# Last 12 of 22 k tiles of the second feed-forward product: seven products of quarters in place of eight

## The chip, the cores and the metric

One core of a Trainium2 chip runs the whole program. The metric is the device time of one execution in microseconds (us); the kernel before takes 709.41 us (median of 3 runs, 708.23 to 709.94). Engines are named as in the profile: PE is the matrix engine (PEld its weight loads), DVE the vector engine, ACT the scalar engine, POOL the GpSimd engine, SP the engine that issues most DMAs.

## The reference

One decoder layer on x of 512 tokens by 1024 channels: two token mixers (a convolution and a forgetting attention) with an output projection, then a feed-forward block. The change touches the last line:

```
x  = x + merged @ w_out                     # mixers
h2 = rmsnorm(x, g_ffn)
gu = h2 @ w_ffn_in                          # 1024 -> 2 x 2816
x  = x + (silu(gu[:, :2816]) * gu[:, 2816:]) @ w_ffn_out     # 2816 -> 1024
```

Everything is float32. A product is made of three passes in the rounded type that PE takes (fp32r): an operand is split in a high part (rounded) and a low part (the rest), and high x high, high x low and low x high are added up in PSUM (`mm3`, `split`).

## The kernel before

Programs for the five engines are written in one order by hand (a manual schedule); each engine takes its instructions in that order and waits on semaphores. Two wrappers, `V` and `T`, stand for DVE and PE, so all their instructions have line L147.

**First feed-forward product.** It is already made in quarters, seven products for eight (Winograd's form), for 11 column groups m of 256 hidden channels in each half. `seq` lists the products (m, p), and for each `one(n)` runs `product` (24 matmuls of 256 columns) and `combine`, which takes results out of PSUM: c11, c12 and c22 hold partial results, and `act` the silu times gate, transposed (128 hidden channels by 512 tokens) for 22 tiles. The last five products are those of m = 10: P6, P5, P7, P3, P4. P7 and P4 add into the same PSUM bank X: after P7 DVE reads X (`c<-acc,c`), and P4 may only then go on adding to it. P4's result is read by `act<-c,acc`.

**Second product** (`for k in range(NF)`). Its 22 k tiles of 128 hidden channels each add to all eight PSUM banks (4 token tiles by 2 halves of the 1024 output columns), 24 matmuls of 512 columns a tile, 528 in all. PSUM has two tags of four banks, `acc` and `mx`, and the banks are taken in the order acc, acc, mx, mx, acc, acc, mx, mx; the sixth is the X of m = 10. For tile k, `down_load` brings 128 rows of w_ffn_out (`wd`, tag raw), `down_split` makes `wdh` (ACT) and `wdl` (DVE), and `act_split` makes `ah` (ACT) and `al` (DVE) of one `act` tile. The weights have three buffers of each tag, so the split for tile k + 2 waits until tile k - 1 is done. The first three loads and splits stand between the last five products of `seq`. In the last tile each finished bank is added to x1 (`x<-x,acc`, `x<-x,mx`) and stored.

**Memory.** `slot` (26 tiles, tag s2) holds mixers' tiles, c22 and act; `f4` (22 tiles of 4 KB a partition) holds operands of the first product and then ah and al, at 2 KB of their 4 KB.

Of the kernel before, what the change touches and what calls it, by code (L numbers as in the profile page):

```python
# [27 lines left out]
NF = DFF // P  # L28
# [7 lines left out]
def hybrid_layer(ctx, tc, x, g_mix, w_in, b_forget, w_dw, b_dw, g_ln, b_ln, w_conv_out,  # L36
# [3 lines left out]
    nc = tc.nc  # L40
    A, G = nc.scalar, nc.gpsimd

    x, out = x[0], out[0]
    w_in, w_conv_out, w_attn_out = w_in[0], w_conv_out[0], w_attn_out[0]
    w_out, w_ffn_in, w_ffn_out = w_out[0], w_ffn_in[0], w_ffn_out[0]

    keep = ctx.enter_context(tc.tile_pool(name="keep", bufs=1))
    wp = ctx.enter_context(tc.tile_pool(name="wp", bufs=2))  # L50
    big = ctx.enter_context(tc.tile_pool(name="big", bufs=1))
    sm = ctx.enter_context(tc.tile_pool(name="sm", bufs=4))
    ps = ctx.enter_context(tc.tile_pool(name="ps", bufs=4, space=bass.MemoryType.PSUM))
    side = tc.alloc_tile_pool(name="side", bufs=1, side="right", reuse_waits="tile")
    ctx.enter_context(tc.manual_schedule())

# [4 lines left out]
        return ps.tile([P, n], F32, tag="mx", name="mx")  # L61

    def slot(dt=F32, name="s2"):
        return big.tile([P, 542], dt, tag="s2", bufs=26, name=name)

    def g8(dt=F32, name="g8"):
        return side.tile([P, 4, 512], dt, tag="g8", bufs=5, name=name)
# [93 lines left out]
    V, T = Clocked(nc.vector, v_adds), Clocked(nc.tensor, t_adds)  # L161
# [450 lines left out]
    for i in range(2):  # L612
        a_ = side.tile([P, NT, 196], F32R, name=f"sq{i}")
# [222 lines left out]
    x1 = []  # L836
# [116 lines left out]
    B11, B21, B22, T1, T2, T3, T4 = range(7)  # L953
# [73 lines left out]
        b_lo(T4, t4)  # L1027
        b_lo(B22, b22)

    act = [None] * NF  # L1030
    X, Y, Z = {}, {}, {}

    def product(m, p):
        hi, lo = ops_.pop((m, p))
        bh, bl = bop[B_OF[p]]
        new = p in (1, 2, 5)
        if p == 1:
            X[m] = acc()
        elif p == 2:
            Z[m] = mx()  # L1040
        elif p == 5:
            Y[m] = mx()
        o = Z[m] if p == 2 else Y[m] if p in (3, 5) else X[m]
        for f in range(2):
            fs = slice(f * P, f * P + P)
            for w in range(3):
                for k in range(KH):

                    first = new and f + w + k == 0
                    T.matmul(o[:, f * 256:f * 256 + 256], (hi, hi, lo)[w][:, k, fs], (bh, bl, bh)[w][:, k, :],  # L1050
                             start=first, stop=w == 2 and k == KH - 1, skip_group_check=not (new and f == 0))

    c11, c12, c22 = {}, {}, {}

    def combine(m, p):
        if p == 1:
            c11[m] = wk(name="c11")
            A.copy(c11[m], X[m])
        elif p == 2:
            V.tensor_tensor(c11[m], Z[m], c11[m], op=ALU.add)  # L1060
            A.activation(c11[m], c11[m], AF.Silu)
        elif p == 5:
            c22[m] = slot(name="c22")[:, :S]
            A.copy(c22[m], Y[m])
        elif p == 6:
            c12[m] = wk(name="c12")
            A.copy(c12[m], X[m])
        elif p == 7:
            V.tensor_tensor(c22[m], X[m], c22[m], op=ALU.add)
        elif p == 4:  # L1070
            for i in range(2):
                if act[2 * m + i] is None:
                    act[2 * m + i] = slot(name="act")[:, :S]
                hs = slice(i * 256, i * 256 + 256)
                V.tensor_tensor(act[2 * m + i][:, :256], c11[m][:, hs], X[m][:, hs], op=ALU.mult)
        elif p == 3:
            V.tensor_tensor(c12[m], Y[m], c12[m], op=ALU.add)
            A.activation(c12[m], c12[m], AF.Silu)
            for i in range(2):
                if act[2 * m + i] is None:  # L1080
                    act[2 * m + i] = slot(name="act")[:, :S]
                hs = slice(i * 256, i * 256 + 256)
                V.tensor_tensor(act[2 * m + i][:, 256:], c12[m][:, hs], c22[m][:, hs], op=ALU.mult)

    def prep_first():

# [15 lines left out]
    def one(n):  # L1102
        product(*seq[n])
        combine(*seq[n])


    down, acts = {}, {}

    def d_rows(k):
        return w_ffn_out[k * P:(k + 1) * P, :]  # L1110

    def down_load(k):
        if k < NF:
            raw = wp.tile([P, D], F32, tag="raw", bufs=3, name="wd")
            nc.sync.dma_start(raw, d_rows(k))
            down[k] = raw

    def down_split(k):
        if k < NF:
            raw = down[k]  # L1120
            hi = wp.tile([P, D], F32R, tag="whi", bufs=3, name="wdh")
            lo = wp.tile([P, D], F32R, tag="wlo", bufs=3, name="wdl")
            split(hi, lo, raw)
            down[k] = hi, lo

    def act_split(k):
        if k < NF:
            hi, lo = f4(F32R, "ah"), f4(F32R, "al")
            hi, lo = (t.rearrange("p k c -> p (k c)")[:, :S] for t in (hi, lo))
            split(hi, lo, act[k])  # L1130
            acts[k] = hi, lo


    for m in range(NP):
# [30 lines left out]
    for n in range(NS):  # L1165
        early = n < 3
        if early:
            for fn, args in todo[n]:
                fn(*args)
        for th in tokens.get(n, ()):  # L1170
            th()
        if not early:
            for fn, args in todo[n]:
                fn(*args)
        for m, key in loads.get(n, ()):
            f_load(m, key)
        one(n)
        if n >= NS - 5:
            i = n - NS + 5
            if i < 3:  # L1180
                down_load(i)
            if 0 < i < 4:
                down_split(i - 1)
            if 1 < i < 4:
                act_split(i - 2)
    banks = [(acc, acc, mx, mx)[i % 4]() for i in range(8)]
    for k in range(NF):
        down_load(k + 3)
        if k > 0:
            down_split(k + 2)  # L1190
        act_split(k + 2)
        hi, lo = down[k]
        for i in range(8):
            t, c = divmod(i, 2)
            ts, cs = slice(t * P, (t + 1) * P), slice(c * 512, (c + 1) * 512)
            mm3(banks[i], acts[k][0][:, ts], acts[k][1][:, ts], hi[:, cs], lo[:, cs], k == 0, k == NF - 1)
            if k == NF - 1:
                V.tensor_tensor(x1[t][:, cs], x1[t][:, cs], banks[i], op=ALU.add)
                nc.sync.dma_start(out[t * P:(t + 1) * P, cs], x1[t][:, cs])
    side.release()  # L1200


# [23 lines left out]
```

## Time and profile before

| | us |
|---|---|
| median of 3 runs | 709.41 |
| the profiled execution, device time | 708.81 |
| its span, first to last instruction | 707.0 |
| PE busy | 694.7 |
| DVE busy | 459.9 |
| ACT busy | 371.6 |
| POOL busy | 123.3 |

The profile follows one execution; times in it are counted from its first instruction. A row of the timeline gives start, duration, engine, line, operation, output and inputs, and in brackets how long the engine had been idle and who ended it. Ends of matmuls are modelled: two matmuls that follow each other overlap in the rows, so their rate is read from their starts. `wd`, `wdh`, `wdl` are a tile of w_ffn_out, its high and its low part; `ah`, `al` those of the activations; `c` any of c11, c12, c22.

### The profile page before, as it was taken

The page shows a single profiled execution, that of the slowest core. Times are in us where ns is not written, and L with a number is a line of the kernel's source. Part 1 is how long each engine was busy: PE and PEld are TensorE (multiplying, and loading weights), DVE is VectorE, ACT ScalarE, POOL GpSimd, SP SyncE. Part 2 cuts the span into 40 slices and gives each one's busy share as a digit, 9 for nine tenths or more (in the row PEclk, how much of TensorE's full clock was granted, in tenths as well). Part 3 has the DMA queues.
Part 4 walks back from the last instruction along what each step waited for, and adds up shares of the span by engine and source line. Part 5 has one row for each costly group of instructions (what it writes and reads, how often), then busy time and mean ns, then how long its engine had stood idle before and what let it go on. Part 6 is the DMA issues. An engine that isn't in the chain of part 4 may idle for free. (4 is left out here: it accounts for less than half of the span.)

```text
span 707.0 us, 10716 instructions
## 1 busy us (share of the span) xinstructions
PE 694.7 (98%) x4264; PEld 614.8 (87%) x4264; DVE 459.9 (65%) x736; ACT 371.6 (53%) x585; POOL 123.3 (17%) x138
## 2 busy tenths in 40 slices
PE   6999999999999999999999999999999999999997
PEld 5988879888888888887889999999999987888886
DVE  5579985988773568497677677667667663333333
ACT  5424546487788677553567465665555552223320
POOL 1302257243333221210001011111110100000000
PEclk9999999999999999999999999999999999999999
DMA  8438999366656611295016568777667463332203
GB/s 257 95 104 172 186 188 184 91 131 125 120 120 122 141 68 60 89 328 177 1 61 131 137 150 179 150 160 162 155 145 158 61 176 93 105 101 90 89 31 119
DMA packets 67124, 92.13 MB, mean 130 GB/s; under 512 B 3281, under 2 KB 46289, under 8 KB 67074
## 3 DMA queue, kind: packets, MB, share of 16 engines
q1 hardware_dynamic: 47810, 65.58, 30.5%
q0 software_dynamic: 18976, 25.35, 22.6%
q8 instruction: 33, 0.54, 0.3%
q10 hardware_dynamic: 288, 0.52, 0.2%
q14 instruction: 17, 0.14, 0.1%
HBM read 89.34 MB, written 2.10 MB: 129 GB/s over the span
## 5 line engine op out<-in xcount | busy, mean ns | idle before, releaser
L212 ACT CAST whi<-wraw 128x1024 fp32r<-128x1024 f32 (+1 forms) x52 | 54.4, 1049 | 54.6 <-PE acc L147 35.4
L147 DVE SCALAR_TENSOR_TENSOR cv<-apad,prm,cv 128x512 f32<-128x512 f32 x120 | 83.1, 764 | 0.0
L147 PE MATMUL acc<-hT_hi,whi 128*128 128x512 f32 (+1 forms) x208 | 75.6, 384 | 0.7 <-ACT hT_hi L77 0.7
L147 DVE TENSOR_TENSOR wdl<-wd,wdh 128x1024 fp32r<-128x1024 f32 x22 | 27.0, 1226 | 74.5 <-ACT wdh L77 74.5
L147 PE MATMUL acc<-hT_hi,wlo 128*128 128x512 f32 (+1 forms) x208 | 73.1, 371 | 0.0
L147 PE MATMUL acc<-hT_lo,whi 128*128 128x512 f32 (+1 forms) x208 | 73.0, 370 | 0.0
L147 DVE TENSOR_TENSOR wl<-wA,wh 128x1024 fp32r<-128x1024 f32 x46 | 56.1, 1222 | 20.0 <-ACT wh L928 19.6
L928 ACT CAST wh<-wA 128x1024 fp32r<-128x1024 f32 x66 | 68.1, 1046 | 1.0 <-DVE wA L147 0.6
L77 ACT CAST wdh<-wd 128x1024 fp32r<-128x1024 f32 x22 | 23.0, 1048 | 79.0 <-PE mx L147 69.3
L924 POOL DMA_DIRECT2D wl<-in_w_ffn_in_dram x20 | 25.7, 1286 | 181.8 <-PE mx L147 105.5
L147 PE MATMUL acc<-bl,wh 128*128 128x256 f32 x352 | 56.3, 282 | 0.0
L147 PE MATMUL acc<-bh,wh 128*128 128x256 f32 x352 | 56.2, 281 | 0.0
L147 PE MATMUL acc<-bh,wl 128*128 128x256 f32 x352 | 56.1, 281 | 0.0
L147 DVE TENSOR_TENSOR wlo<-wraw,whi 128x1024 fp32r<-128x1024 f32 x28 | 34.3, 1223 | 22.1 <-ACT whi L212 21.3
L147 PEld LDWEIGHTS acc<-bl,wh 128*128 128x128 f32 x352 | 48.0, 188 | 0.1
L147 PEld LDWEIGHTS acc<-bh,wh 128*128 128x128 f32 x352 | 47.9, 188 | 0.1
L147 PEld LDWEIGHTS acc<-bh,wl 128*128 128x128 f32 x352 | 47.9, 188 | 0.0
L218 POOL DMA_DIRECT2D wlo<-in_w_in_dram x24 | 29.1, 1213 | 89.1 <-ACT wlo L216 72.0
L147 PEld LDWEIGHTS acc<-hT_hi,wlo 128*128 128x128 f32 x208 | 38.0, 191 | 7.2
L147 PE MATMUL acc<-wlo,hT_hi 128*128 128x512 f32 (+2 forms) x128 | 43.4, 339 | 0.4 <-DMA wlo<-in_w_in_dram 0.4
L147 PEld LDWEIGHTS acc<-hT_hi,whi 128*128 128x128 f32 x208 | 38.1, 193 | 6.5 <-ACT hT_hi L77 1.1
L147 PE MATMUL acc<-whi,hT_lo 128*128 128x512 f32 (+2 forms) x128 | 43.4, 339 | 0.0
(222 smaller groups left out, 1675.1 us busy)
## 6 DMA issues: line engine op xcount, KB each, us to landing
wA<-in_w_ffn_in_dram SPq DMA_DIRECT2D x44, 512.0 KB, 3.8
wraw<-in_w_in_dram SPq DMA_DIRECT2D x26, 512.0 KB, 3.9
wlo<-in_w_in_dram POOLq DMA_DIRECT2D x22, 512.0 KB, 7.9
wd<-in_w_ffn_out_dram SPq DMA_DIRECT2D x22, 512.0 KB, 3.3
wl<-in_w_ffn_in_dram POOLq DMA_DIRECT2D x20, 512.0 KB, 8.4
wraw<-in_w_in_dram SPq DMA_DIRECT2D x16, 256.0 KB, 3.7
wraw<-in_w_out_dram SPq DMA_DIRECT2D x8, 512.0 KB, 6.2
wraw<-in_w_attn_out_dram SPq DMA_DIRECT2D x4, 512.0 KB, 3.4
```

Of the source, the lines that this page charges most:

```text
L77: A.copy(hi, src)
L147: return f(out, *args, **kw)
L212: A.copy(hi, raw)
L218: G.dma_start(lo[:, :, at:at + d["n"]], w_rows(d, c0), accum_op=ALU.add)
L924: G.dma_start(lo, w_quarter(m, *WHERE[SRC[p]]), accum_op=ALU.add)
L928: A.copy(hi, wq[m, SRC[p]])
```

## The change

The 22 k tiles are now 10 plain tiles (KS) and three groups q of four (NQ = 3). In a group the activations (512 tokens by 512 channels) and the weights (512 by 1024) are cut in quarters, and seven products of quarters (P1, P5, P6, P2, P7, P3, P4 for q = 0, 1, 2 each: 21 steps of 12 matmuls of 512 columns) give what eight would. Sums of quarters (S1 to S4 of activations, T1 to T4 of weights) are made by DVE, in place except S1 and T1. Quarters of w_ffn_out are loaded as `dB..` tiles during the plain tiles. Each step's operands are prepared three steps ahead: `dh` and the high part of `da` by ACT, the low part of `da` and `dl` by DVE. For P2 and P3 the low part `dlo` is made five steps ahead by a negated copy (ACT) and a DMA from POOL that adds the quarter again. Results stay in PSUM over steps: X for P1, P6, P7, P4, Y for P5 and P3, Z for P2; after the last group `add_out` adds them to x1.

`act` becomes 11 tiles of two k tiles each, in a new pool on the bytes of the `slot` pool, which is released after product n = 6. So the silu-times-gate product is one instruction of 128x2x256 where there were two of 128x256, and `act_split` works on 128x1024 for two k tiles. For m < 2 c22 is taken from X after P7 instead of from Y after P5.

```diff
-    act = [None] * NF
+    act = [None] * NP
+    def t512(name):
+        return pools["act"].tile([P, 512], F32, tag="t512", bufs=5, name=name)
+    def act_of(m): ...
+            act[m] = pools["act"].tile([P, 2, 512], F32, tag="act", bufs=NP, name="act")
...
-        elif p == 5:
-            c22[m] = slot(name="c22")[:, :S]
+        elif p == 5 and m > 1:
+            c22[m] = t512("c22")
...
         elif p == 7:
-            V.tensor_tensor(c22[m], X[m], c22[m], op=ALU.add)
+            if m < 2:
+                c22[m] = t512("c22")
+                A.copy(c22[m], X[m])
+                V.tensor_tensor(c22[m], Y[m], c22[m], op=ALU.add)
+            else:
+                V.tensor_tensor(c22[m], X[m], c22[m], op=ALU.add)
         elif p == 4:
-            for i in range(2): ...
-                V.tensor_tensor(act[2 * m + i][:, :256], c11[m][:, hs], X[m][:, hs], op=ALU.mult)
+            V.tensor_tensor(act_of(m)[:, :, :256], two(c11[m]), two(X[m]), op=ALU.mult)
...
-    def act_split(k):
-        if k < NF:
-            hi, lo = f4(F32R, "ah"), f4(F32R, "al")
-            split(hi, lo, act[k])
+    NQ = 3
+    KS = NF - 4 * NQ
+    def act_split(m):
+        if 2 * m < KS:
+            acts[m] = f2(F32R, "ah"), f2(F32R, "al")
+            split(*acts[m], act[m])
...
+    Q_SUM = {"T1": ("B12", "B11", "T1"), "T2": ("B22", "T1", "T1"), "T3": ("B22", "B12", "B12"), "T4": ("B21", "T1", "B21"),
+             "S1": ("A21", "A22", "S1"), "S2": ("S1", "A11", "A11"), "S3": ("A11", "A21", "A21"), "S4": ("A12", "A11", "A12")}
...
+    A_SRC = {1: "A11", 2: "A12", 3: "A12", 4: "A22", 5: "S1", 6: "A11", 7: "A21"}
+    B_SRC = {1: "B11", 2: "B21", 3: "B22", 4: "B21", 5: "T1", 6: "T1", 7: "B12"}
+    d_seq = [(p, q) for p in (1, 5, 6, 2, 7, 3, 4) for q in range(NQ)]
+    def wq_slot(dt, name):
+        tag = ("raw", "raw", "whi", "wlo", "raw", "whi", "wlo", "whi", "wlo")[d_n[0] % 9]
...
+    def q_neg(p, q):
+        lo_q[p, q] = f2(F32R, "dlo")
+        A.activation(lo_q[p, q], dq[q, B_SRC[p]], AF.Copy, scale=-1.0)
+        G.dma_start(lo_q[p, q], q_rows(q, B_SRC[p]), accum_op=ALU.add)
+    def q_ops(p, q):
+        w = dq[q, B_SRC[p]]
+        hi = wq_slot(F32R, "dh")
+        lo = lo_q[p, q] if (p, q) in lo_q else wq_slot(F32R, "dl")
+        a_op = f2(F32R, "da")
+        A.copy(hi, w)
+        A.copy(two(a_op[:, 0, :]), quarter(q, A_SRC[p]))
+        V.tensor_tensor(two(a_op[:, 1, :]), quarter(q, A_SRC[p]), two(a_op[:, 0, :].bitcast(F32)), op=ALU.subtract)
+        if (p, q) not in lo_q:
+            V.tensor_tensor(lo, w, hi.bitcast(F32), op=ALU.subtract)
+    def q_step(p, q):
+        bank = {1: "X", 2: "Z", 3: "Y", 4: "X", 5: "Y", 6: "X", 7: "X"}[p]
...
+        for i in range(2):
+            for kk in range(2):
+                for w in range(3):
+                    a_ = a_op[:, w == 2, kk * 256 + i * P:kk * 256 + i * P + P]
+                    T.matmul(dbank[bank][i], a_, (hi, lo, hi)[w][:, kk, :], ...)
+            if q == NQ - 1: ... add_out(t, c, dbank[bank][i], p in (2, 3, 7, 4))
...
-            if 1 < i < 4:
-                act_split(i - 2)
+            if i in (1, 3):
+                act_split(i // 2)
...
+        d_plan(KS - 2 if q < 2 else KS - 1, q_ops, 1, q)
+        d_plan(KS - 1, q_sum, q, "S2")
+        d_plan(KS + q, q_ops, 5, q)
+        d_plan(KS + 1 + q, q_sum, q, "T2")
+        d_plan(KS + d_at[2, q] - 5, q_neg, 2, q)
+        d_plan(KS + d_at[3, q] - 5, q_neg, 3, q)
+        for p in (6, 2, 7, 3, 4):
+            d_plan(KS + d_at[p, q] - 3, q_ops, p, q)
...
-    for k in range(NF): ...
-        act_split(k + 2)
+    for k in range(KS): ...
+        if k % 2 == 0 and k > 0:
+            act_split(k // 2 + 1)
+        for fn, args in d_todo[k]:
+            fn(*args)
...
+    for n, (p, q) in enumerate(d_seq):
+        for fn, args in d_todo[KS + n]:
+            fn(*args)
+        q_step(p, q)
```

The first place is DVE between the last products of the first feed-forward product and the second. Before (`c_6171` is c22 of m = 10, read from X after P7; `c_6138` is c12 after P3; `c_5978` is c11, multiplied with P4's result in `acc`):

```order
L147 TENSOR_TENSOR wdl<-wd,wdh 128x1024
L147 TENSOR_TENSOR c_6171<-acc,c_6171 128x512
L147 TENSOR_TENSOR wdl<-wd,wdh 128x1024
L147 TENSOR_TENSOR al<-act,ah 128x512
L147 TENSOR_TENSOR c_6138<-mx,c_6138 128x512
L147 TENSOR_TENSOR act<-c_6138,c_6171 128x256 x2
L147 TENSOR_TENSOR wdl<-wd,wdh 128x1024
L147 TENSOR_TENSOR al<-act,ah 128x512
L147 TENSOR_TENSOR act<-c_5978,acc 128x256 x2
```

The same place on DVE after the change (`c_6148` is c22, `c_6115` c12, `c_5958` c11):

```order
L149 TENSOR_TENSOR wdl<-wd,wdh 128x1024
L149 TENSOR_TENSOR al<-act,ah 128x1024
L149 TENSOR_TENSOR c_6148<-acc,c_6148 128x512
L149 TENSOR_TENSOR wdl<-wd,wdh 128x1024
L149 TENSOR_TENSOR c_6115<-mx,c_6115 128x512
L149 TENSOR_TENSOR act<-c_6115,c_6148 128x2x256
L149 TENSOR_TENSOR wdl<-wd,wdh 128x1024
L149 TENSOR_TENSOR al<-act,ah 128x1024
L149 TENSOR_TENSOR act<-c_5958,acc 128x2x256
```

The first low part of the activations, now twice as long, has moved up in front of the read of X for c22; the second one, also twice as long, stands as before in front of the read of P4's result.

The second place is DVE where the plain tiles end and the steps begin, after the change; before, the eight `x` rows were the kernel's last (`x_0` to `x_3` are x1's token tiles, `da`, `dl` operands of P1 and P5, `dT` sums of weights):

```order
L149 TENSOR_TENSOR da_6592<-act_6051,da_6592 128x512
L149 TENSOR_TENSOR dl_6591<-dB11_6337,dh_6590 128x1024
L149 TENSOR_TENSOR act_6051<-dS1_6412,act_6051 128x2x256
L149 TENSOR_TENSOR x1_0_3298<-x1_0_3298,acc_6254 128x512
L149 TENSOR_TENSOR x1_0_3298<-x1_0_3298,acc_6255 128x512
L149 TENSOR_TENSOR x1_1_3300<-x1_1_3300,mx_6256 128x512
L149 TENSOR_TENSOR x1_1_3300<-x1_1_3300,mx_6257 128x512
L149 TENSOR_TENSOR x1_2_3302<-x1_2_3302,acc_6258 128x512
L149 TENSOR_TENSOR x1_2_3302<-x1_2_3302,acc_6259 128x512
L149 TENSOR_TENSOR x1_3_3304<-x1_3_3304,mx_6260 128x512
L149 TENSOR_TENSOR x1_3_3304<-x1_3_3304,mx_6261 128x512
L149 TENSOR_TENSOR da_6632<-dS1_6334,da_6632 128x512
```

The first two adds set free the two banks that P1 writes, and operands of P1 and a sum stand in front of them; all eight stand in front of the operands of P5.

## Rows read from the trace of the kernel before

**Rows 1.** The page: busy time of engines, and the chain that ended last

```profile
PE 694.7 (98%) x4264; PEld 614.8 (87%) x4264; DVE 459.9 (65%) x736; ACT 371.6 (53%) x585; POOL 123.3 (17%) x138
...
PE 16%; DVE 1%; issue 0%
```

**Rows 2.** Busy us (and instructions) by stretch: PE, PEld, DVE, ACT, POOL, then clock, DMA

```profile
300.00:320.00 20.00, 20.00 (x89) 16.21 (x88) 17.99 (x22) 11.97 (x15) 3.07 (x5) 1.00 0.94 322
380.00:400.00 20.00, 20.00 (x171) 20.00 (x170) 12.44 (x16) 11.47 (x14) 2.57 (x2) 1.00 0.79 179
450.00:500.00 50.00, 50.00 (x424) 50.00 (x423) 35.87 (x40) 27.68 (x34) 5.13 (x4) 1.00 0.75 164
584.00:704.00 120.00, 119.28 (x513) 96.20 (x513) 40.72 (x47) 29.83 (x38) 0.00 (x0) 1.00 0.26 87
```

**Rows 3.** Timeline, second product's beginning and end (start us, us, engine, line, operation)

```profile
578.92 0.39 PE L147 MATMUL acc<-wdh,ah 128*128 128x512 f32 x1
...
582.15 0.40 PE L147 MATMUL acc<-wdh,al 128*128 128x512 f32 x1
...
583.95 0.51 PE L147 MATMUL acc<-wdh,ah 128*128 128x512 f32 x1 [1.40 <-DVE act L147]
...
702.62 1.38 DVE L147 TENSOR_TENSOR x<-x,mx 128x512 f32<-128x512 f32 x2
...
702.88 0.40 PE L147 MATMUL mx<-wdh,al 128*128 128x512 f32 x1
```

**Rows 4.** Timeline, last products of the first feed-forward product, DVE, ACT and PEld

```profile
573.89 1.04 ACT L928 CAST wh<-wA 128x1024 fp32r<-128x1024 f32 x1
574.02 1.23 DVE L147 TENSOR_TENSOR wdl<-wd,wdh 128x1024 fp32r<-128x1024 f32 x1 [2.50 <-ACT wdh L77]
...
575.16 0.68 DVE L147 TENSOR_TENSOR c<-acc,c 128x512 f32<-128x512 f32 x1
...
575.96 0.54 PEld L147 LDWEIGHTS acc<-bh,wh 128*128 128x128 f32 x4
...
576.26 1.05 ACT L77 CAST wdh<-wd 128x1024 fp32r<-128x1024 f32 x1 [1.32 <-PE mx L147]
...
577.34 1.22 DVE L147 TENSOR_TENSOR wdl<-wd,wdh 128x1024 fp32r<-128x1024 f32 x1 [1.49 <-ACT wdh L77]
...
580.34 1.03 ACT L77 CAST wdh<-wd 128x1024 fp32r<-128x1024 f32 x1
...
581.40 1.23 DVE L147 TENSOR_TENSOR wdl<-wd,wdh 128x1024 fp32r<-128x1024 f32 x1 [0.18 <-ACT wdh L77]
...
582.55 0.68 DVE L147 TENSOR_TENSOR al<-act,ah 128x512 fp32r<-128x512 f32 x1
...
583.15 0.75 DVE L147 TENSOR_TENSOR act<-c,acc 128x256 f32<-128x256 f32 x2
```

**Rows 5.** Groups of instructions from 584 us on: count, busy us, mean ns, idle before

```profile
L147 DVE TENSOR_TENSOR wdl<-wd,wdh 128x1024 fp32r<-128x1024 f32 x19 | 23.3, 1226 | 70.3 <-ACT wdh L77 70.3
L77 ACT CAST wdh<-wd 128x1024 fp32r<-128x1024 f32 x19 | 19.9, 1048 | 75.9 <-PE mx L147 68.0 <-issue 7.9
...
L147 DVE TENSOR_TENSOR al<-act,ah 128x512 fp32r<-128x512 f32 x20 | 13.7, 685 | 0.0
L77 ACT CAST ah<-act 128x512 fp32r<-128x512 f32 x19 | 11.7, 616 | 0.0
```

**Rows 6.** Tile wl from 400 to 580 us: POOL's adding DMAs, and their landing

```profile
L924 POOL DMA_DIRECT2D wl<-in_w_ffn_in_dram x17: 1273/1282/1303, 407.1 to 564.7; - x17
...
DMA to landing us min/median/max: 6.0/8.5/10.3
```

**Rows 7.** Timeline of PE in the output projection, six matmuls apart

```profile
317.66 0.39 PE L147 MATMUL mx<-wlo,mhi 128*128 128x512 f32 x1
...
319.05 0.39 PE L147 MATMUL mx<-wlo,mhi 128*128 128x512 f32 x1
```

**Rows 8.** The page, DMA issues by queue: KB each, median us to landing

```profile
wA<-in_w_ffn_in_dram SPq DMA_DIRECT2D x44, 512.0 KB, 3.8
```

More of the change, by code (lines that the diff above doesn't have):

```diff
@@ L53, in hybrid_layer @@
     ps = ctx.enter_context(tc.tile_pool(name="ps", bufs=4, space=bass.MemoryType.PSUM))
+    s2p = tc.alloc_tile_pool(name="s2p", bufs=1, reuse_waits="tile")
     side = tc.alloc_tile_pool(name="side", bufs=1, side="right", reuse_waits="tile")
@@ L63, in slot @@
     def slot(dt=F32, name="s2"):
-        return big.tile([P, 542], dt, tag="s2", bufs=26, name=name)
+        return s2p.tile([P, 542], dt, tag="s2", bufs=26, name=name)
     def g8(dt=F32, name="g8"):
@@ L1028, in norm2, with act_of, two @@
         b_lo(B22, b22)
-    act = [None] * NF
+    act = [None] * NP
+    pools = {}
+    def t512(name):
+        return pools["act"].tile([P, 512], F32, tag="t512", bufs=5, name=name)
+    def act_of(m):
+        if act[m] is None:
+            act[m] = pools["act"].tile([P, 2, 512], F32, tag="act", bufs=NP, name="act")
+        return act[m]
+    def two(t):
+        return t.rearrange("p (f c) -> p f c", f=2)
     X, Y, Z = {}, {}, {}
@@ L1068, in combine @@
         elif p == 7:
-            V.tensor_tensor(c22[m], X[m], c22[m], op=ALU.add)
-        elif p == 4:
[L1071 to L1074, printed above, removed]
-                V.tensor_tensor(act[2 * m + i][:, :256], c11[m][:, hs], X[m][:, hs], op=ALU.mult)
+            if m < 2:
[4 more added lines that the diff above has]
+                V.tensor_tensor(c22[m], X[m], c22[m], op=ALU.add)
+        elif p == 4:
+            V.tensor_tensor(act_of(m)[:, :, :256], two(c11[m]), two(X[m]), op=ALU.mult)
         elif p == 3:
@@ L1078, in combine @@
             A.activation(c12[m], c12[m], AF.Silu)
[L1079 to L1083, printed above, removed]
+            V.tensor_tensor(act_of(m)[:, :, 256:], two(c12[m]), two(c22[m]), op=ALU.mult)
     def prep_first():
@@ L1104, in one @@
         combine(*seq[n])
+    NQ = 3
+    KS = NF - 4 * NQ
     down, acts = {}, {}
-    def d_rows(k):
-        return w_ffn_out[k * P:(k + 1) * P, :]
     def down_load(k):
-        if k < NF:
+        if k < KS:
             raw = wp.tile([P, D], F32, tag="raw", bufs=3, name="wd")
-            nc.sync.dma_start(raw, d_rows(k))
+            nc.sync.dma_start(raw, w_ffn_out[k * P:(k + 1) * P, :])
             down[k] = raw
     def down_split(k):
-        if k < NF:
+        if k < KS:
             raw = down[k]
@@ L1124, in down_split, with f2 @@
             down[k] = hi, lo
-    def act_split(k):
-        if k < NF:
-            hi, lo = f4(F32R, "ah"), f4(F32R, "al")
-            hi, lo = (t.rearrange("p k c -> p (k c)")[:, :S] for t in (hi, lo))
-            split(hi, lo, act[k])
-            acts[k] = hi, lo
+    def act_split(m):
+        if 2 * m < KS:
+            acts[m] = f2(F32R, "ah"), f2(F32R, "al")
+            split(*acts[m], act[m])
+    def f2(dt=F32, name="f2"):
+        return f4(dt, name).rearrange("p k c -> p (k c)").rearrange("p (k c) -> p k c", k=2)
@@ new lines, in hybrid_layer, with q_rows, q_load @@
+    dq, lo_q, d_ops = {}, {}, {}
+    def q_rows(q, key):
+        k0, c0 = (KS // 2 + 2 * q + int(key[1]) - 1) * 256, (int(key[2]) - 1) * 512
+        return w_ffn_out[k0:k0 + 256, c0:c0 + 512].rearrange("(k p) c -> p k c", p=P)
+    def q_load(q, key):
+        dq[q, key] = f2(name="d" + key)
+        nc.sync.dma_start(dq[q, key], q_rows(q, key))
+    Q_SUM = {"T1": ("B12", "B11", "T1"), "T2": ("B22", "T1", "T1"), "T3": ("B22", "B12", "B12"), "T4": ("B21", "T1", "B21"),
+             "S1": ("A21", "A22", "S1"), "S2": ("S1", "A11", "A11"), "S3": ("A11", "A21", "A21"), "S4": ("A12", "A11", "A12")}
@@ new lines, in quarter, with q_sum @@
+    def quarter(q, key):
+        if key[0] == "A":
+            ts = slice((int(key[1]) - 1) * 256, int(key[1]) * 256)
+            return act[KS // 2 + 2 * q + int(key[2]) - 1][:, :, ts]
+        return dq[q, key]
+    def q_sum(q, key):
+        a, b, o = Q_SUM[key]
+        if key == "T1":
+            dq[q, o] = f2(name="dT1")
+        elif key == "S1":
+            dq[q, o] = two(t512("dS1"))
+        V.tensor_tensor(quarter(q, o), quarter(q, a), quarter(q, b), op=ALU.add if key == "S1" else ALU.subtract)
@@ new lines, in hybrid_layer @@
+    A_SRC = {1: "A11", 2: "A12", 3: "A12", 4: "A22", 5: "S1", 6: "A11", 7: "A21"}
+    B_SRC = {1: "B11", 2: "B21", 3: "B22", 4: "B21", 5: "T1", 6: "T1", 7: "B12"}
+    d_seq = [(p, q) for p in (1, 5, 6, 2, 7, 3, 4) for q in range(NQ)]
+    d_at = {s_: n for n, s_ in enumerate(d_seq)}
+    d_n = [0]
+    def wq_slot(dt, name):
+        tag = ("raw", "raw", "whi", "wlo", "raw", "whi", "wlo", "whi", "wlo")[d_n[0] % 9]
+        d_n[0] += 1
+        return wp.tile([P, D], dt, tag=tag, bufs=3, name=name).rearrange("p (k c) -> p k c", k=2)
@@ new lines, in q_neg @@
+    def q_neg(p, q):
[12 more added lines that the diff above has]
+            V.tensor_tensor(lo, w, hi.bitcast(F32), op=ALU.subtract)
+        d_ops[p, q] = hi, lo, a_op
@@ new lines, in q_step @@
+    def q_step(p, q):
+        hi, lo, a_op = d_ops.pop((p, q))
+        bank = {1: "X", 2: "Z", 3: "Y", 4: "X", 5: "Y", 6: "X", 7: "X"}[p]
+        new = q == 0 and p in (1, 2, 5)
+        if new:
+            dbank[bank] = [{"X": acc, "Y": mx, "Z": acc}[bank]() for _ in range(2)]
+        for i in range(2):
+            for kk in range(2):
+                for w in range(3):
+                    a_ = a_op[:, w == 2, kk * 256 + i * P:kk * 256 + i * P + P]
+                    T.matmul(dbank[bank][i], a_, (hi, lo, hi)[w][:, kk, :], start=new and kk + w == 0,
+                             stop=q == NQ - 1 and kk == 1 and w == 2, skip_group_check=p not in (1, 2, 5))
+            if q == NQ - 1:
+                for t, c in {1: ((i, 0),), 2: ((i, 0),), 6: ((i, 1),), 3: ((i, 1),), 5: ((2 + i, 1),),
+                             7: ((2 + i, 1),), 4: ((2 + i, 0),)}[p]:
+                    add_out(t, c, dbank[bank][i], p in (2, 3, 7, 4))
@@ L1134, in hybrid_layer, with add_out @@
+    dbank = {}
+    def add_out(t, c, bank, last):
+        cs = slice(c * 512, (c + 1) * 512)
+        V.tensor_tensor(x1[t][:, cs], x1[t][:, cs], bank, op=ALU.add)
+        if last:
+            nc.sync.dma_start(out[t * P:(t + 1) * P, cs], x1[t][:, cs])
     for m in range(NP):
@@ L1177, in hybrid_layer @@
         one(n)
+        if n == 6:
+            assert not Line.threads
+            s2p.release()
+            pools["act"] = tc.alloc_tile_pool(name="act", bufs=1, reuse_waits="tile")
         if n >= NS - 5:
@@ L1183, in hybrid_layer, with d_plan @@
                 down_split(i - 1)
-            if 1 < i < 4:
-                act_split(i - 2)
+            if i in (1, 3):
+                act_split(i // 2)
     banks = [(acc, acc, mx, mx)[i % 4]() for i in range(8)]
-    for k in range(NF):
+    d_todo = [[] for _ in range(KS + len(d_seq))]
+    def d_plan(n, fn, *args):
+        d_todo[n].append((fn, args))
+    for q in range(NQ):
+        for i, key in enumerate(("B11", "B12", "B22", "B21")):
+            d_plan(2 * i + q, q_load, q, key)
+        d_plan(2 + q, q_sum, q, "S1")
+        d_plan(2 + q, q_sum, q, "S3")
+        d_plan(5 + q, q_sum, q, "T1")
+        d_plan(6 + q, q_sum, q, "T3")
+        d_plan(KS - 2 if q < 2 else KS - 1, q_ops, 1, q)
[6 more added lines that the diff above has]
+            d_plan(KS + d_at[p, q] - 3, q_ops, p, q)
+        d_plan(KS + d_at[2, q] - 2, q_sum, q, "S4")
+        d_plan(KS + d_at[2, q] - 1, q_sum, q, "T4")
+    for k in range(KS):
         down_load(k + 3)
@@ L1195, in hybrid_layer @@
             ts, cs = slice(t * P, (t + 1) * P), slice(c * 512, (c + 1) * 512)
[L1196 to L1199, printed above, removed]
+            mm3(banks[i], *(o[:, k % 2, ts] for o in acts[k // 2]), hi[:, cs], lo[:, cs], k == 0, k == KS - 1)
+            if k == KS - 1:
+                add_out(t, c, banks[i], False)
+    for n, (p, q) in enumerate(d_seq):
+        for fn, args in d_todo[KS + n]:
+            fn(*args)
+        q_step(p, q)
+    pools["act"].release()
     side.release()
```

## The prediction

> **What bounds the kernel now.** I read the page first: PE is busy 98% of the span, and the chain that ended last is PE for all but 1% of what it shows [rows 1]. So a matmul taken away is worth its time, as long as nothing else makes PE wait in its place. The view of stretches then shows what room the others have in the part that is changed: from 584 to 704 us PE is busy 119.28 of 120 us, DVE only 40.72 and ACT 29.83, with no POOL work and DMA at a quarter [rows 2]. The timeline gives the stage's two ends: its first matmul starts at 578.92 and its last at 702.88, and there is one gap: after the matmul at 582.15 the next starts at 583.95, held by DVE's `act` [rows 3]. 528 matmuls make 527 distances. Call the distance d: the gap is 583.95 - 582.15 - d, so 702.88 - 578.92 = 526 d + 1.80, and d = 0.2322 us. The gap beyond a normal distance is 1.57. The rows' durations of 0.39 are longer because matmuls overlap; only starts count.
>
> **The term that pays.** Plain tiles keep 10 x 24 = 240 matmuls of 512 columns, the steps have 21 x 12 = 252: 492 for 528, 36 fewer. The new ones have the same shape, with a new weight load each, as before. 36 x 0.2322 = 8.36 us. Is d the same where DVE is busier? In the output projection DVE works 17.99 of 20 us [rows 2], and there six matmuls take 319.05 - 317.66 = 1.39, or 0.2317 each [rows 7]. I take d as it is, with both ends of the doubt at 0.4 us (492 x 0.0008, the difference between 0.2322 and about 0.233, either way).
>
> Here the Trainium skill has another figure: its page "TensorE: Matmul & The Clock Gate", section Back-to-back issue gap, gives about 131 ns per matmul for a sustained stream of loads and matmuls of 512 columns. By that the 36 would be worth 4.7 us; the starts in this trace, in a stretch without a gap, do not agree with it, and decide.
>
> **The handover between the two products.** This is where the change puts work on the path. Today: DVE makes the first `wdl` at 574.02, reads X for c22 at 575.16 to 575.84, and P4 begins at 575.96, so P4 has a tenth of a microsecond to spare [rows 4]. Now `al` of 128x1024 stands between the two. The trace has that operation as `wdl`: 1.226 long [rows 5], with the next instruction 1.14 after its start [rows 4]. ACT makes `ah` where `wh` stood at 573.89, and is done by 575.0. So the read of X moves to 576.30 to 576.98, and P4 to 577.10: **PE waits 1.14 us that it did not wait.** ACT's `wh` for P4 moves behind `ah`, to about 575.9, still in time.
>
> The old gap then shrinks. The first matmul of the second product moves to 580.06, and its sixth bank could start at 582.38 + 1.14 = 583.52. That bank needs P4's result read by `act`. On the way stand the third `wdh`, which waits for P4's end as the second waited for P3's (576.26, 0.30 after 575.96): 579.96 + 0.30 = 580.26; `wdl` 1.06 later (580.34 to 581.40 today) at 581.32; `al`, now long, at 582.47; `act` 1.14 later at 583.61, one instruction of 0.69 in place of two in 0.75 (no row has 128x2x256; 512 columns in one are 0.685, in two 0.75, so 0.06 is the doubt); the bank at 584.35 [rows 4, 5]. So PE waits 0.83 where it waited 1.57, and the sixth bank starts 584.35 - 583.95 = **0.40 later** than today. Bounds: if neither wait shows, -1.57; if the new wait comes in full and the second stays with a long `al` on top, 1.14 + 0.60 = +1.74. I take +0.40, since every link has its row.
>
> **The plain tiles.** Tile 1 starts at 584.35 + 9 d = 586.44; a tile is 5.573, tile 9 ends at 636.60, and 21 steps of 2.786 end at 695.1. In each tile DVE now does a `wdl`, half a long `al` and two sums: at most 1.23 + 0.61 + 2.45 = 4.3 of 5.57. The eighth to tenth tiles have more, P1's operands and S2. I followed DVE from the last split (ready 0.30 after tile 6 ends at 619.86, so `wdl` at 621.2), with 1.14 a long and 0.60 a short instruction (582.55 to 583.15 [rows 4]) and waits for ACT and for free buffers: it reaches the first add of a finished bank at 633.8, and the bank is free at 634.4. P1 needs it at 636.60: 2.2 us to spare. The twelve weight quarters are on SP from tile 0 to 8; the nearest load lands in 3.8 us [rows 8] and each has some three tiles (17 us) before its sum. The early tiles' changes (one `act` instruction for two, c22 of m = 0 and 1 by way of ACT) lie under a PE that does not wait there: m = 0 and 1 fall between 380 and 400, where PE is busy all 20 us, DVE 12.44 and ACT 11.47, and 450 to 500 reads alike [rows 2]. If ACT's copy were late, X would be free 0.6 us later, with a whole product in between. Cost 0.
>
> **The steps.** From the end of tile 9 DVE has 18 `da`, 12 `dl`, six sums of weights, three of activations, 12 adds before the end, and 2 us of adds left over: 18 x 0.685 + 12 x 1.226 + 6 x 1.226 + 3 x 0.685 + 12 x 0.69 + 2 = 46.7 of 58.5 us. ACT has 18 x (1.05 + 0.62) + 6 x 1.05 = 36.4 [rows 5]. Both are below PE. What matters then is order: the eight adds end at 638.6, P5's three operands follow by 646.2 (the third is needed at 650.5), P6's first by 649.1 (needed 653.3). Counting full durations instead of starts takes away about 1.5 of these 4. Buffers: nine weight slots in rotation free a slot three steps before its new content is needed. The stores' tail is the same pair of adds and last store, 4.1 us from 702.88 to the span's end; cost 0.
>
> The six adding DMAs are the tightest. The third one of P2 waits for ACT behind the last T2 (650.3), two `dh`, two `da` and the negated copy, 4.4 us: it starts at 654.7, POOL takes 1.28 to issue, and landing takes 6.0 to 10.3 [rows 6]: 666.3 at worst, needed at 636.60 + 11 x 2.786 + d = 667.5. I take it as hidden, with 1 us to spare at worst and 3 at the median.
>
> The Trainium skill warns of just this: page "SBUF — State Buffer", in its box on DVE blocking DMA, says that a DMA issued from GpSimd can be starved while DVE runs in a mode that takes both port pairs. The same page says under Who interferes with whom that a two-tensor operation has no such mode; DVE runs only those here, and DMAs from POOL landed in 6.0 to 10.3 us with DVE busy 72%, so the trace agrees that it is not starved by them.
>
> **Sum.** -8.36 + 0.40 = -7.96. The profiled execution took 708.81 (span 707.0 and 1.8 around it), so 700.85 for such a one; the median of the runs is 0.60 above it, and 709.41 - 7.96 = **701.4**.
>
> **Rivals.**
> 1. *Late low parts.* A DMA of P2 or P3 lands late, or DVE reaches the first add late. If landing beside the loaded DVE took double the median, 17 us, the third of P2 would come at 673.0, 5.5 after its need: 706.9. For: only 1 us to spare at worst. Against: [rows 6] were measured with DVE at 72% and DMA three times as busy, here it is quiet.
> 2. *No gain.* d rises in the steps, because six matmuls in a row go to one bank and DVE and ACT write beside them. To cancel all, 252 matmuls would need 7.96 / 252 = 0.032 more each, 0.264: 709.4. Against: [rows 7], six in one bank, with DVE at 90%.
> 3. *Slower.* The preparation loses its lead of three steps, and each step waits for its own chain: `dh` 1.05, `da` high 0.62, `da` low 0.69, `dl` 1.23 = 3.59 for 2.79. That is 0.80 on each of the 12 steps that make a `dl`, 9.6 us, and the six sums of weights on the same chain add 6 x 1.23 = 7.4: 701.4 + 17.0 = 718.4. It decides from the point where DVE comes to P6 more than 4 us late, for then no step has its operands early. For: eight adds stand in front of P5's operands. Against: DVE has 11.8 us of room over the steps and would catch up.
>
> That the 36 matmuls do not go is ruled out by the order of PE.
>
> **How the numbers follow.** My forecast 0.80; late low parts 0.10; no gain 0.05; slower 0.05. Its own range is 699.1 (no wait at the handover, -8.36 - 1.57, and 0.4 of d) to 703.2 (-8.36 + 1.74, and 0.4 of d). A measurement here tells 0.3%, 2.1 us, from no change: faster means below 707.3, which the forecast and the first rival are: 0.90. Same 0.05, slower 0.05. Both ends at once are unlikely; to hold 8 in 10 with some of the first rival I take 699.6 to 704.8.
>
> **What would show it.** PE: 492 matmuls of 512 columns, the first near 580.1, a wait near 1.1 us before P4 ended by DVE's `c`, one near 0.8 before the sixth bank ended by `act`, then none to the last start near 694.9. Steps 2.79 apart. DVE busy about 47 us in the steps, with waits of its own for PE's buffers. It would be wrong if PE waits in the steps: for `da` or `dl` (third rival), for a DMA (first), or if d is above 0.235 (second).

## The result and the profile after

| | before | changed |
|---|---|---|
| median of 4 runs each (before: the three above and one more), us | 709.57 (708.23 to 709.94) | 701.21 (699.41 to 702.04) |
| ratio, 95% interval | | 0.9882 (0.9859 to 0.9906) |
| profiled execution, its span | 708.81, 707.0 | 700.93, 699.1 |
| first feed-forward matmul to last matmul, starts | 355.32 to 702.88: 347.56 | 355.36 to 695.00: 339.64 |

The kernel is 8.4 us faster by the medians. In the two traces the stretch from the first feed-forward matmul to the last is 7.92 us shorter. I call it the stage and compare it in all that follows: what lies ahead of it differs between executions (the same changed kernel came to its first feed-forward matmul at 355.36 in one trace, with a granted clock of 0.51 from 333.0 to 336.4 us, and at 354.10 in another, e8, with 1.00 there). It has nothing to do with the change: up to the stage the instructions of PE, DVE, ACT and POOL are the same in both kernels.

The page of the changed kernel, busy time of each engine, answers to [rows 1]:

```profile
PE 688.2 (98%) x4228; PEld 609.1 (87%) x4228; DVE 495.8 (71%) x759; ACT 390.8 (56%) x604; POOL 130.5 (19%) x144
```

36 matmuls fewer; DVE has 36 us more to do, ACT 19, POOL 7, and PE is still at 98%. Now the view of waits, PE from 570 us to the end (total, times, longest):

```profile
PE acc L149 <- DVE c L149: 0.9, 1, 0.9
PE acc L149 <- DVE act L149: 0.6, 1, 0.6
```

These two are all. Both lie at the handover, and none is in the steps. The timeline of the handover in the changed kernel (start, duration, engine, operation) answers to [rows 3, 4]:

```profile
575.15 1.22 DVE L149 TENSOR_TENSOR al<-act,ah 128x1024 fp32r<-128x1024 f32 x1
576.28 0.68 DVE L149 TENSOR_TENSOR c<-acc,c 128x512 f32<-128x512 f32 x1
577.11 0.71 PE L149 MATMUL acc<-bh,wh 128*128 128x256 f32 x4 [0.91 <-DVE c L149]
...
580.05 0.39 PE L149 MATMUL acc<-wdh,ah 128*128 128x512 f32 x1
...
581.33 1.23 DVE L149 TENSOR_TENSOR wdl<-wd,wdh 128x1024 fp32r<-128x1024 f32 x1 [0.79 <-ACT wdh L79]
582.47 1.22 DVE L149 TENSOR_TENSOR al<-act,ah 128x1024 fp32r<-128x1024 f32 x1
583.61 0.68 DVE L149 TENSOR_TENSOR act<-c,acc 128x512 f32<-128x512 f32 x1
...
584.35 0.50 PE L149 MATMUL acc<-wdh,ah 128*128 128x512 f32 x1 [0.60 <-DVE act L149]
...
695.00 0.39 PE L149 MATMUL acc<-dh,da 128*128 128x512 f32 x1
```

DVE reads X (`c<-acc,c`) only behind the long `al`, and P4 begins behind that. The chain that ended last, from the first step on (start, length, what), shows the steps back to back:

```profile
636.84 8.40 PE acc L149 x36
645.23 8.41 PE mx L149 x36
653.64 25.05 PE acc L149 x108
678.69 8.35 PE mx L149 x36
687.04 8.36 PE acc L149 x36
```

The stretch of the steps (columns as in [rows 2]) says how much room is left beside PE:

```profile
636.00:695.00 59.00, 59.00 (x256) 47.63 (x254) 44.39 (x57) 31.81 (x40) 7.16 (x6) 1.00 0.40 81
```

### The profile page after: what moved, and what is told of

The parts are those of the page before. It is cut to its first block, busy times and chain, and to the rows that moved or that the text cites. A ratio compares the mean times of both kernels' runs of the same rounds, so it can differ in the third digit from the quotient of the medians.

```text
span 699.1 us, 10700 instructions
## 1 busy us (share of the span) xinstructions
PE 688.2 (98%) x4228; PEld 609.1 (87%) x4228; DVE 495.8 (71%) x759; ACT 390.8 (56%) x604; POOL 130.5 (19%) x144
## 4 chain that ended last, share of the span: by engine, by line
PE 94%; DVE 2%; ACT 2%; issue 1%; DMA 1%; POOL 0%; SPq 0%; ACTq 0%
PE acc L149 64%; PE mx L149 30%; DMA x<-in_x_dram 1%; ACT wh L930 0%; DVE h L149 0%; DVE bl L149 0%; DVE x L149 0%; DVE al L149 0%; ACT junk L353 0%; ACT wdh L79 0%; DVE wdl L149 0%; ACT bh L988 0%; DVE wl L149 0%; DVE hr L149 0%; ACT hr L985 0%
## 5 line engine op out<-in xcount | busy, mean ns | idle before, releaser
L149 PE MATMUL acc<-whi,hT_hi 128*128 128x512 f32 (+2 forms) x128 | 43.4, 339 | 0.0
L149 PE MATMUL mx<-bl,wh 128*128 128x256 f32 x264 | 42.3, 282 | 1.0 <-DVE bl L149 1.0
```

The costliest lines, as they stand in the source:

```text
L149: return f(out, *args, **kw)
```

## The experiments

Ratios are to the kernel before, run on the same chip. The changed kernel's stage is 339.64 us, that of before 347.56. Each stage is read from one profiled execution; the changed kernel profiled again (e8) gave 339.77, so a tenth or two of a microsecond between two stages says little.

| run | median us | ratio (95%) | stage us |
|---|---|---|---|
| e1_nq2 | 705.18 | 0.9943 (0.9924 to 0.9962) | 343.46 |
| e2_nq0 | 709.68 | 1.0004 (0.9990 to 1.0018) | 347.94 |
| e3_read_first | 699.99 | 0.9880 (0.9859 to 0.9902) | 339.08 |
| e4_handover | 698.22 | 0.9852 (0.9830 to 0.9874) | 337.78 |
| e5_no_lead | 712.59 | 1.0052 (1.0036 to 1.0067) | 349.77 |
| e6_low_by_dve | 701.89 | 0.9903 (0.9886 to 0.9920) | 339.76 |
| e7_late_low | 701.49 (1 run) | | 339.88 |
| e8_change_again | 700.09 | 0.9889 (0.9865 to 0.9913) | 339.77 |
| e9_handover_again | 698.19 | 0.9861 (0.9835 to 0.9887) | 337.55 |
| e10_late_low | 705.42 | 0.9954 (0.9935 to 0.9973) | 345.74 |

### What the fewer matmuls are worth: two groups in steps, or none

```
-    NQ = 3
+    NQ = 2                          # e1: 14 plain tiles, 14 steps
```

> Two groups of four k tiles in place of three (14 plain tiles, 14 steps), all else as in the change. Theory (each group takes away 12 matmuls of 512 columns at 0.2322 us, and nothing else of the steps shows): 12 x 0.2322 = 2.79 us slower than the changed kernel, about 704.0 against 701.2, and 5.2 faster than the kernel before; no wait of PE in the steps. Rival (the steps cost something of their own, hidden in part): the difference from the changed kernel is clearly below 2.8 us.

Measured: a stage 3.82 longer than with three groups, 1.03 more than the 12 matmuls. The timeline of e1 shows where part of it went, in the steps of P5 and P6:

```profile
667.82 1.22 DVE L149 TENSOR_TENSOR dl<-dT,dh 128x1024 fp32r<-128x1024 f32 x1
...
669.10 0.50 PE L149 MATMUL mx<-dl,da 128*128 128x512 f32 x1 [0.41 <-DVE dl L149]
...
674.34 0.63 PE L149 MATMUL acc<-dh,da 128*128 128x512 f32 x2
674.97 0.50 PE L149 MATMUL acc<-dl,da 128*128 128x512 f32 x1
```

With two groups a product has two steps, and operands prepared three steps ahead are those of another product: P6's stand in front of P5's second in the order of ACT and DVE, and wait for T2. PE then waits by its starts some 0.7 us here, at P5's second step, and 0.3 at P6's second, about 1.0 together. So the price of a matmul stands, but that the preparation costs nothing holds for the spacing of three groups, not in general. My expectation missed that.

```
-    NQ = 3
+    NQ = 0                          # e2: all 22 tiles plain; the pair tiles
-        add_out(t, c, banks[i], False)
+        add_out(t, c, banks[i], NQ == 0)   # and the handover stay as changed
```

> No group at all: 22 plain tiles, so of the change only the pair tiles of act on the mixers' bytes, the longer act splits and c22 of m = 0 and 1 remain. Theory (these cost only at the handover between the two products): sixth bank of the second product at 584.35 us where it was 583.95, P4 waits about 0.9 us for the read of X, the kernel 0.4 us slower than before, about 710.0. Rival (pair tiles give part of the gain): faster than the kernel before by more than 0.5 us.

Measured: a stage 0.38 longer than before, and the same time by its interval. The timeline of e2 has the two waits of the changed kernel, so they come with the pair tiles and not with the steps:

```profile
576.14 0.71 PE L149 MATMUL acc<-bh,wh 128*128 128x256 f32 x4 [0.91 <-DVE c L149]
...
583.36 0.50 PE L149 MATMUL acc<-wdh,ah 128*128 128x512 f32 x1 [0.66 <-DVE act L149]
```

e2 and the changed kernel have the same handover and differ in the steps alone: 347.94 - 339.64 = 8.30 us for 36 matmuls, 0.231 each. That is the gain by itself, and what it lacks of the 36 x 0.2322 = 8.36 is no more than two stages of the same kernel differ by.

### The handover: X read first, and then P4's result too

```
-            if i in (1, 3): act_split(i // 2)
+            if i == 2: act_split(0)        # ahead of down_split(i - 1)
+            if i == 3: act_split(1)
```

> The changed kernel with the first split of act moved behind the read of X for c22, so that P4 does not wait; the second split stays where it is. Theory (the sixth bank is bound by a chain of its own, through the third weight split and the second split of act): P4's wait goes, the sixth bank starts at about 583.8 in place of 584.35, so 0.5 us faster than the changed kernel, though a wait of 1.1 us has gone. Rival (each wait of PE counts in full): sixth bank near 583.2, 1.1 us faster.

Measured: 0.56 less in the stage, as half of the wait would give and not the whole 1.1. The timeline of e3:

```profile
574.36 0.65 PE L149 MATMUL acc<-bh,wh 128*128 128x256 f32 x4
...
580.24 1.22 DVE L149 TENSOR_TENSOR al<-act,ah 128x1024 fp32r<-128x1024 f32 x1
581.38 0.68 DVE L149 TENSOR_TENSOR act<-c,acc 128x512 f32<-128x512 f32 x1
582.11 0.50 PE L149 MATMUL acc<-wdh,ah 128*128 128x512 f32 x1 [1.19 <-DVE act L149]
```

P4 no longer waits, but the sixth bank does, for 1.19 where it was 0.60: the long `al` in front of `act` now ends last. The wait moved. So e4 moves that one too:

```
+            if i == 2: act_split(0)
-            if 0 < i < 4: down_split(i - 1)
+            if i in (1, 2, 4): down_split((0, 1, None, 2)[i - 1])
-            if i in (1, 3): act_split(i // 2)
+            if i == 4: act_split(1)
```

> As the one before, and the third weight split and the second split of act moved behind the read of P4's result. Theory: no wait of PE left at the handover, sixth bank at about 582.4, 1.97 us faster than the changed kernel: about 699.2; tile 2, whose operands come later now, does not wait, since it starts near 590. Rival: tile 1 or 2 waits for the moved splits and takes the gain back.

The timeline of e4 has no wait of PE from P4 to the end:

```profile
574.55 0.65 PE L149 MATMUL acc<-bh,wh 128*128 128x256 f32 x4
...
577.42 0.39 PE L149 MATMUL acc<-wdh,ah 128*128 128x512 f32 x1
...
578.96 0.68 DVE L149 TENSOR_TENSOR act<-c,acc 128x512 f32<-128x512 f32 x1
579.56 1.22 DVE L149 TENSOR_TENSOR wdl<-wd,wdh 128x1024 fp32r<-128x1024 f32 x1
580.69 1.22 DVE L149 TENSOR_TENSOR al<-act,ah 128x1024 fp32r<-128x1024 f32 x1
...
580.96 0.39 PE L149 MATMUL acc<-wdh,ah 128*128 128x512 f32 x1
```

`act` now comes ahead of the third `wdl` and of the second `al`, and P4's result is read before its bank, the sixth, is due at 580.96. The stage is 1.86 shorter than the changed kernel's. That this is a gain beside the changed kernel, on one chip, is what the next two are for:

> The changed kernel once more, to be compared with the next on one chip: about 8 us faster than the kernel before, sixth bank 7.2 us after P4's first matmul.

> The version without waits at the handover once more. Theory: 1.9 us faster than the changed kernel on the same chip, near 10 us faster than the kernel before. Rival (the difference of the first time was the execution's beginning, not the handover): the same as the changed kernel.

The changed kernel is again faster than the one before, by 8.35 us, with 7.2 us from P4 to the sixth bank. The version without waits: 698.19 against 700.09, 1.9 us, and 2.22 in the stage, of which 2.0 lie ahead of the sixth bank. The two ratios to before, 0.9861 and 0.9889, have intervals that overlap (0.9865 to 0.9887), but the slowest run of this version there, 699.36, lies below the fastest of the changed kernel, 699.65; the stage and the missing waits carry the claim more than the medians do. This version is faster than both kernels.

### The steps: no lead, no adding DMAs, late adding DMAs

```
-            d_plan(KS + d_at[p, q] - 3, q_ops, p, q)
+            d_plan(KS + d_at[p, q], q_ops, p, q)    # e5; S4, T4 at KS + d_at[2, q]
```

> The changed kernel with the operands of P6, P2, P7, P3 and P4 made right before their step in the engines' orders, not three steps ahead (P1 and P5, and the DMAs for the low parts, as they are). Theory (the three steps of lead are what hides 47 us of DVE work): at each of the five borders the two adds of the step before now stand in front of the next operands, so PE waits two adds, da and dl, about 3.2 us before P6, P7 and P4, and two adds and da, about 1.7 us, before P2 and P3: 13 us in all, about 714, slower than the kernel before. Rival (the engines run ahead of PE anyway, since waits are by buffer and not by order): no wait, 701.

Measured: slower than before, by 2.2 us in the stage and 3.5 by the medians. The profiled execution is the fastest of the ten, and its granted clock in the steps is 1.00; six of the others had a lower mean clock than any run of either kernel (last section), so the median may hold more than these waits. The timeline of e5 shows PE's five waits:

```profile
654.48 0.51 PE L149 MATMUL acc<-dl,da 128*128 128x512 f32 x1 [2.29 <-DVE dl L149]
...
664.28 0.73 PE L149 MATMUL acc<-dh,da 128*128 128x512 f32 x2 [0.91 <-DVE da L149]
...
674.96 0.50 PE L149 MATMUL acc<-dl,da 128*128 128x512 f32 x1 [2.28 <-DVE dl L149]
...
684.76 0.74 PE L149 MATMUL mx<-dh,da 128*128 128x512 f32 x2 [0.91 <-DVE da L149]
...
695.44 0.50 PE L149 MATMUL acc<-dl,da 128*128 128x512 f32 x1 [2.28 <-DVE dl L149]
```

They stand where a product begins whose operands DVE makes behind the adds of the product before, and by the starts of matmuls, the late one right behind each wait included, make up the 10.1 us by which the stage is longer than the changed kernel's, where I had said 13: of the two adds in front of each `da`, the one of the first bank is done while PE still works on the second. The chain that ended last in e5 has one add only at such a place:

```profile
652.00 0.69 DVE x L149
652.69 0.60 DVE da L149
653.29 1.15 DVE dl L149
```

So the third rival's mechanism exists, at the five borders and not in every step, and the lead of three steps keeps it away.

```
-        d_plan(KS + d_at[2, q] - 5, q_neg, 2, q)      # e6: both lines go; DVE makes
-        d_plan(KS + d_at[3, q] - 5, q_neg, 3, q)      # all the low parts
```

> The changed kernel with the low parts of P2 and P3 made by DVE, as for the other products, and no DMA from POOL in the steps. Theory (DVE has room in the steps, and the DMAs are not on the path): DVE 7.3 us more in the steps, PE waits for nothing there, time as the changed kernel within 0.5 us. Rival (DVE is near its limit, and the DMAs are what keeps it below): PE waits several us before P2, P7 or P3.

Measured: a stage 0.12 longer, no wait of PE in the steps. The stretch of the steps in e6:

```profile
636.00:695.00 59.00, 59.00 (x255) 47.57 (x254) 51.06 (x64) 26.50 (x34) 0.00 (x0) 1.00 0.07 27
```

DVE takes the six subtractions and has 8 of 59 us left. The adding DMAs are not needed for the time.

> The changed kernel with the negated copy for the DMAs of P2 and P3 one step ahead in order in place of five. With the landing of 5.6 us that the changed kernel shows, the low part of the first P2 comes at 661.6 (needed 662.0), of the second at 664.8 (needed 664.8), of the third at 667.5 (needed 667.6): under 1.5 us of waits in all. Rival (landing near 8.5 us as in the first product): waits of 2 to 3 us at P2 and again at P3, 4 to 6 us in all.

This one failed as an experiment. It moved the two lines above from five steps ahead to one; but the operands are made three steps ahead, found no low part there, and DVE made it, so the six DMAs filled tiles that nothing read. Its 339.88 says only that six unused DMAs cost at most 0.24 us, in one run. The test was made properly in e10, where the operands take the tile and leave it to the DMA:

```
-        lo_q[p, q] = f2(F32R, "dlo")                  # in q_neg
...
-        lo = lo_q[p, q] if (p, q) in lo_q else wq_slot(F32R, "dl")
+        lo = lo_q.setdefault((p, q), f2(F32R, "dlo")) if p in (2, 3) else wq_slot(F32R, "dl")
...
-        d_plan(KS + d_at[2, q] - 5, q_neg, 2, q)      # and the same for P3
+        d_plan(KS + d_at[2, q] - 1, q_neg, 2, q)
```

> The negated copies and the adding DMAs of P2 and P3 are ordered one step ahead of their product where the change has five; the step's operands, three steps ahead, take the tile and leave it to the DMA to fill. So POOL issues the six DMAs some four steps (11 us) later, beside a chip that is otherwise the same. First rival of the prediction made real. If landing takes 5.6 us, as the six took in the changed kernel, the low parts of P2's three steps come at about 661.6, 664.8 and 667.5 us of the changed kernel's time, needed at 662.0, 664.8 and 667.6 by the matmuls that read them: waits under 1.5 us in all, a stage of 339.7 to 341.2 us, 700 to 702.5 in the median. If landing takes 8.5 us, the median of the first product's adding DMAs in the kernel before, each of the two products makes PE wait 2 to 3 us: a stage of 343.5 to 346 and a time of 704.5 to 707.

Measured: a stage 6.1 longer, at the upper end of what the slower landing would give, though four of the six DMAs landed in 5.6 to 5.8 (the other two, both for P3, in 6.6 and 8.3). The view of waits of e10, PE (the rows of the steps), and the chain at the second step of P2 and at the last of the three steps of P3:

```profile
PE mx L149 <- DMA dlo<-in_w_ffn_out_dram: 2.6, 1, 2.6
...
PE acc L149 <- DMA dlo<-in_w_ffn_out_dram: 1.0, 1, 1.0
```

```profile
660.21 5.75 DMA dlo<-in_w_ffn_out_dram
...
680.26 8.30 DMA dlo<-in_w_ffn_out_dram
688.56 0.04 issue
688.61 4.17 PE mx L149 x11
```

Three things that I had not reckoned with make up the difference. The second DMA of P2 was issued at 660.21, a good microsecond later than by my count, since ACT's negated copies stand behind the high parts. The last DMA of P3 took 8.30, beside the DMA before it (issued at 677.26, landed at 682.94) and two stores of P7's finished tiles (issued at 679.32 and 680.71). And behind that wait PE ran slowly: 11 matmuls in 4.00 us by their starts (688.61 to 692.61) where 2.56 is normal, 1.44 more. By starts the wait at P2 is 1.1 and that at P3 2.75; with the slow matmuls and small delays at other steps that makes the 6.

## Why the prediction was right

701.4 was forecast, 701.21 measured; within the trace -7.96 was forecast and -7.92 measured, and the terms hold one by one. That the medians agree to 0.2 us is in part luck: four runs of one kernel lie 1.7 (before) and 2.6 us (changed) apart. What carries the account is the stage and its terms.

**The 36 matmuls.** Forecast 8.36. From the sixth bank to the last start the changed kernel has 476 distances in 695.00 - 584.35 = 110.65, or 0.2325 each, and before 512 in 702.88 - 583.95 = 118.93, or 0.2323: 8.28 less. DVE beside them does not stretch them by more than 0.0002 each, where the second rival needed 0.032. The 131 ns of the Trainium skill's "TensorE: Matmul & The Clock Gate", section Back-to-back issue gap, do not fit this stretch either.

**The handover.** Forecast +0.40, measured from the stage's start to the sixth bank 228.99 against 228.63, +0.36. The links came where the working had them (the two stages begin within 0.04 us of each other, at 355.32 and 355.36, so the times can be compared): P4 at 577.11 (577.10 forecast), the first matmul of the second product at 580.05 (580.06), the sixth bank at 584.35 (584.35). The doubt about one instruction of 128x2x256 is settled: `act` takes 0.68. That the term is the two waits, and that one moves into the other, e3 and e4 show.

**The steps.** No wait was forecast and none came. DVE's first plain add, from the changed kernel's timeline, stands at 633.73 (633.8 forecast), and the eight adds end where P5's first `da` follows them (638.6 forecast):

```profile
633.73 1.28 DVE L149 TENSOR_TENSOR x<-x,acc 128x512 f32<-128x512 f32 x2
...
638.51 0.69 DVE L149 TENSOR_TENSOR da<-dS,da 128x512 fp32r<-128x512 f32 x1
```

DVE's 44.39 us and ACT's 31.81 are a little under the 46.7 and 36.4 forecast; ACT has 40 instructions in the stretch where I counted 42, and some of P1's operands were ready before it. That order, and not busy time, decides there was right: e5 has as much DVE work and loses 10 us. That "hidden" was argued too generally shows in e1.

**The loads and adding DMAs were the mis-sized terms.** For a weight quarter I took the 3.8 us of [rows 8], and for an adding DMA 6.0 to 10.3 of [rows 6]. The page after has them, out<-in, queue, count, KB and median us to landing:

```profile
dB<-in_w_ffn_out_dram SPq DMA_DIRECT2D x12, 512.0 KB, 5.5
```

and the adding DMAs' own view, with the third issue of P2, in its timeline of POOL:

```profile
654.79 1.19 POOL L1192 DMA_DIRECT2D dlo<-in_w_ffn_out_dram  x1 [5.73 <-DVE x L149]
```

```profile
DMA to landing us min/median/max: 5.6/5.6/5.9
```

The issue time was right (654.7 forecast); the landing, at 660.7 with the longest of the six, lies 7 us ahead of the need, where I had 1 to 3. Part of that was a slip in the sum: the view counts a landing from the start of its issue (e10's last one from 680.26, where POOL's issue starts, to 688.56), so POOL's 1.28 went in twice. By [rows 6] the third low part was due at 665.0 at worst, 2.5 us ahead of the need. DVE was busy 75% of the stretch, and the six landed in 5.6 to 5.9 us. That agrees with the Trainium skill, page "SBUF — State Buffer", Who interferes with whom, by which two-tensor operations did not stall a DMA as copies did. The first rival's mechanism is real nevertheless: with the DMAs four steps later, e10 takes 705.42. That this lies near the 706.9 worked out for it is chance: the rival had one landing of 17 us and a wait of 5.5, and e10 has waits of 1.1 and 2.75 and 1.44 of slow matmuls. The third rival's mechanism is real too, with a stage 10.1 longer in e5 where it had 17.0: it had a wait in each of 12 steps and the sums of weights on top, and only five places wait.

## What to carry to other kernels

Where PE bounds a stage without gaps, a matmul taken away is worth its distance between starts, and the work that pays for it is free only as far as its order is: take the lead away, with the same work for DVE, and 7.9 us of gain in the stage become a loss of 2.2. A wait at a handover moves to the next reader when one instruction is moved out of its way; follow the chain to the next bank before counting it, and move both. Test "it is hidden" at another size as well: here two groups in place of three were enough to uncover a wait.

## What the runs showed of the hardware that was not expected

In the profiled execution of e10 the matmuls are slow for a while behind the wait for a late DMA. The stretches of e10 around the wait (columns as in [rows 2]; the eighth figure, behind POOL's, is the granted clock):

```profile
685.60:688.60 3.00, 0.42 (x2) 0.00 (x0) 0.29 (x1) 0.00 (x0) 0.00 (x0) 0.93 0.44 79
688.60:689.60 1.00, 0.99 (x2) 0.83 (x3) 0.00 (x0) 0.00 (x0) 0.00 (x0) 0.50 0.00 0
689.60:690.60 1.00, 1.00 (x4) 0.78 (x3) 0.00 (x0) 0.00 (x0) 0.00 (x0) 0.50 0.00 0
690.60:691.60 1.00, 1.00 (x4) 0.81 (x3) 0.46 (x1) 0.00 (x0) 0.00 (x0) 0.51 0.00 0
691.60:692.60 1.00, 1.00 (x5) 0.79 (x5) 0.23 (x1) 0.00 (x0) 0.00 (x0) 1.00 0.00 0
```

The clock is granted at 0.50, the lower of its two levels (1.2 GHz for 2.4), for 3 us behind the wait of 2.58 us, and costs 1.44 us beside the wait itself. Whether every execution of e10 has the dip is open: its profiled one took 706.66, at the slow end of its runs (703.92 to 706.79).

What a wait does to the clock is not settled by this. The waits of 2.28 and 2.29 us left it at 1.00 in the profiled execution of e5; but six of e5's ten runs have a mean granted clock of 0.993 to 0.995, lower than any run of the kernel before (0.996 at least) or of the changed one (0.997 at least), and these six are 2.9 to 5.8 us slower than the profiled one. Where their clock fell no trace shows. And it falls without a wait as well: in the changed kernel's profile it is 0.51 from 333.0 to 336.4 us, behind four matmuls of a single row (`mx<-grow,onesr`, 1.98 us in all), where in e8 the same matmuls leave it at 1.00. So one execution's clock does not tell another's.

An adding DMA of 512 KB takes 5.6 to 5.9 us in the changed kernel's steps, also where two are in flight at once (issued at 660.13 and 662.55), a median of 8.5 in [rows 6], and in e10 6.6 and 8.3 for the two that had stores issued within 1 us of their own issue. That points to the stores, but no run here takes them away.
